# The output projection of a hybrid attention layer by Strassen's scheme, seven products for a pair of blocks

## Chip, cores and metric

One core of a Trainium2 chip runs the whole kernel. The metric is device time in microseconds; each engine (TensorE, VectorE, ScalarE, GpSimd, and SyncE, which issues the DMAs) runs its own list of instructions in order.

## What is computed

A decoder layer over 4096 tokens of width 1024. One input projection feeds two branches: sliding-window softmax attention (512 wide) and gated linear attention in chunks (512 wide). Both outputs, gated, stand side by side, go through the output projection, and the result is normalised with the residual:

```python
proj = einsum('bsd,de->bse', x, w_in)
out_a = sliding_window_attention(q_a, k_a, v_a, sinks) * silu(g_a)
o_b = gla_chunked(q_b, k_b, v_b, log_a)          # state carried along the sequence
out_b = rms_norm(o_b) * gla_norm_w * silu(g_b)
mix = einsum('bse,ed->bsd', concatenate([out_a, out_b]), w_out)   # 4096x1024 by 1024x1024
x = layer_norm(ALPHA * x + mix, ln_g, ln_b)
```

## The kernel before

The tokens are cut into 32 blocks of 128. Each matrix product runs on float32 values that are split in two float32r parts, high and low; a product is high by high, high by low and low by high, three matmuls for each 128 rows of the contraction (`project`, L135 to L137). `split` (L100 to L105) makes the parts: ScalarE or GpSimd copies the high part, VectorE or GpSimd subtracts it from the value.

The kernel has three stages, each a loop over the blocks.

The first projects and computes sliding-window attention; `a_out` stores the gated result of a block, transposed, in DRAM (half 0 of `mixd`).

The second computes gated linear attention. In an iteration n it projects block n (bq, bv, bk, bg) and finishes block n-1 between the projections (`b_attn`, `b_state`, `b_update`, `b_out`, `b_store`); `b_store` puts the transposed result in half 1 of `mixd`. VectorE and ScalarE have many short instructions here and GpSimd a few. Its four weight groups lie in SBUF, loaded and split by `load_group` near the end of the first stage, the k columns early in it. In the last iteration the two halves of w_o take the places of the v and g groups: 16 pieces, loaded, copied by ScalarE and subtracted by VectorE or GpSimd.

The third stage is the output projection. For each block it loads the two halves from `mixd` and the residual rows xr, splits (mh, ml), multiplies by the two column halves of w_o (two products py of 24 matmuls of 128x512 each, into PSUM banks that go round in two pairs), and evacuates each half on VectorE with the residual added (y, L756) and statistics taken (L757). Then come the aggregate (L758), the reciprocal root in `rsqrt_eps` (L780 to L785, with ScalarE's Ln and Exp between), the negated mean nb (L771), normalisation on ScalarE (L772), multiplication by ln_g on GpSimd (L773), addition of ln_b on VectorE (L774), and the store. The last block does its final arithmetic on VectorE in two halves (L766, L767).

The order of instructions on each engine is not that of the text alone. A planner takes the program once before it runs, and gives each engine, whenever it is free by the planner's own durations, the ready instruction that stands earliest in the text. What it writes is the order in which the engine then runs, whatever the true durations are; an instruction that waits stops all behind it on its engine. DMAs go through SyncE's one queue in the same manner. Tiles with one tag share a fixed number of buffers (`bufs`); a tile's first writer waits for the last reader of the buffer's earlier use. A PSUM bank is one such buffer of 128x512.

## Time and profile before

| | |
|---|---|
| Median of 3 runs | 1752.09 us (1750.44 to 1753.18) |
| Profiled execution | 1752.42 us, span of its instructions 1750.6 us |
| Busy in the span | TensorE 98%, VectorE 63%, ScalarE 48%, GpSimd 26% |
| Output projection, by the profile | first matmul at 1386.1 us, last at 1742.4 |
| DMA | 120.13 MB, mean 69 GB/s |

A row of the profile names the time or busy time in us, the engine (PE is TensorE's matmul, PEld its weight load, DVE VectorE, ACT ScalarE, POOL GpSimd, SPq SyncE's queue), the line of the kernel, the operation, and the tiles written and read. In brackets stands the idle time of the engine just before, and who ended it. The granted clock is TensorE's, 1.00 for 2.4 GHz. Matmuls are pipelined: a row of 0.39 us does not mean that the next one starts 0.39 us later.

### The profile page before, as it was taken

What the parts mean: (1) busy time and instruction counts of PE and PEld (TensorE: products, weight loads), DVE (VectorE), ACT (ScalarE), POOL (GpSimd) and SP (SyncE); (2) the same over time, 40 slices, a digit from 0 to 9 for tenths busy, and PEclk for the clock granted to TensorE, in tenths of its full rate; (3) what the DMA queues carried; (4) which work ended last, traced back from release to release, by engine and by line L of the source; (5) the groups of instructions that cost most, each with busy time, mean ns of one, the idle gap of its engine ahead of it and who ended that gap; (6) DMA issues with size and microseconds to landing.
All of it is one profiled execution on the core that took longest, in us unless ns stands there. A gap on an engine that the chain in (4) does not pass through costs nothing.

```text
span 1750.6 us, 27011 instructions
## 1 busy us (share of the span) xinstructions
PE 1716.2 (98%) x9722; PEld 1474.6 (84%) x9722; DVE 1094.8 (63%) x2802; ACT 847.9 (48%) x2128; POOL 456.6 (26%) x633
## 2 busy tenths in 40 slices
PE   7999999999999998999999999999999899999998
PEld 6788888888888887888888888888888788888886
DVE  6766666666666677566665565565556755555555
ACT  5555555455555556555555555555555622222221
POOL 3222222222222244322222222222222412222221
PEclk9999999999999999999999999999999899999999
DMA  6211111111111123111111111111111444444442
GB/s 204 91 37 37 37 37 37 43 49 37 37 37 37 37 73 105 37 37 37 38 37 37 37 37 37 37 40 41 37 37 37 156 139 145 144 145 144 145 144 84
DMA packets 65674, 120.13 MB, mean 69 GB/s; under 512 B 22658, under 2 KB 26116, under 8 KB 65540
## 3 DMA queue, kind: packets, MB, share of 16 engines
q1 hardware_dynamic: 65540, 118.41, 20.4%
q8 instruction: 76, 1.25, 0.3%
q14 instruction: 58, 0.48, 0.1%
HBM read 84.76 MB, written 33.62 MB: 68 GB/s over the span
## 4 chain that ended last, share of the span: by engine, by line
PE 57%; DVE 1%; ACT 0%; issue 0%; DMA 0%; POOL 0%; DVEq 0%; POOLq 0%; ACTq 0%
PE py L137 7%; PE py L135 7%; PE py L136 7%; PE bg L135 3%; PE bg L137 3%; PE bg L136 3%; PE bv L135 3%; PE bv L136 3%; PE bv L137 3%; PE bq L135 2%; PE bq L137 2%; PE bq L136 2%; PE bk L137 2%; PE bk L136 2%; PE bk L135 2%; PE to L679 1%
## 5 line engine op out<-in xcount | busy, mean ns | idle before, releaser
L135 PE MATMUL py<-wh,mh 128*128 128x512 f32 x512 | 200.4, 391 | 0.0
L137 PE MATMUL py<-wh,ml 128*128 128x512 f32 x512 | 200.4, 391 | 0.0
L136 PE MATMUL py<-wl,mh 128*128 128x512 f32 x512 | 200.3, 391 | 0.0
L341 POOL TENSOR_SCALAR s<-s,rec 128x256 f32<-128x256 f32 x256 | 123.8, 499 | 280.5 <-DVE ngm L329 217.3
L333 ACT ACTIVATE s<-s,ngm 128x256 f32<-128x256 f32 x256 | 127.2, 498 | 137.7 <-DVE ngm L329 132.9
L773 POOL TENSOR_TENSOR y<-y,lg 128x1024 f32<-128x1024 f32 x31 | 74.2, 2394 | 268.9 <-ACT y L772 253.5
L102 POOL TENSOR_SCALAR xh<-xraw 128x512 fp32r<-128x512 f32 x126 | 79.0, 643 | 229.2 <-PE pg L136 192.0
L316 DVE CUSTOM_DVE_ANT_0 s<-psc,msk 128x256 f32<-128x256 f32 x256 | 98.0, 420 | 31.6 <-PE psc L306 30.6
L105 DVE TENSOR_TENSOR pl<-pt,ph 128x512 fp32r<-128x512 f32 x128 | 85.7, 689 | 50.2 <-ACT ph L100 47.6
L137 PEld LDWEIGHTS py<-wh,ml 128*128 128x128 f32 x512 | 96.8, 189 | 20.0
L136 PEld LDWEIGHTS py<-wl,mh 128*128 128x128 f32 x512 | 96.8, 189 | 20.0
L135 PE MATMUL pg<-wh,xh 128*128 128x512 f32 x256 | 112.8, 440 | 0.8 <-DVE vv L249 0.8
L135 PEld LDWEIGHTS py<-wh,mh 128*128 128x128 f32 x512 | 96.8, 189 | 19.8
L100 ACT CAST ph<-pt 128x512 fp32r<-128x512 f32 x128 | 72.1, 589 | 85.0 <-PE pt L355 83.2
L527 POOL TENSOR_TENSOR qp<-bqs,ee 128x256 f32<-128x256 f32 x32 | 23.6, 738 | 337.3 <-ACT ee L524 324.0
L135 PE MATMUL pq<-wh,xh 128*128 128x512 f32 x256 | 104.9, 410 | 6.1 <-ACT wh L100 6.0
L100 ACT CAST mh<-mr 128x1024 fp32r<-128x1024 f32 x32 | 33.7, 1053 | 154.1 <-PE py L136 154.1
L135 PE MATMUL bg<-wh,xh 128*128 128x512 f32 x256 | 107.2, 419 | 0.0
L137 PE MATMUL pq<-wh,xl 128*128 128x512 f32 x256 | 103.4, 404 | 3.1 <-DVE xl L105 3.1
L135 PE MATMUL bv<-wh,xh 128*128 128x512 f32 x256 | 103.8, 405 | 0.0
L136 PE MATMUL pq<-wl,xh 128*128 128x512 f32 x256 | 103.0, 402 | 0.1
L136 PE MATMUL bv<-wl,xh 128*128 128x512 f32 x256 | 101.0, 395 | 0.0
(221 smaller groups left out, 5077.0 us busy)
## 6 DMA issues: line engine op xcount, KB each, us to landing
xraw<-in_xt_dram SPq DMA_DIRECT2D x64, 512.0 KB
mr<-mx SPq DMA_DIRECT2D x64, 256.0 KB
xr<-in_xn_dram SPq DMA_DIRECT2D x32, 512.0 KB
out_dram<-y SPq DMA_DIRECT2D x31, 512.0 KB
mx<-att SPq DMA_DIRECT2D x32, 256.0 KB
mx<-mb SPq DMA_DIRECT2D x32, 256.0 KB
wraw<-in_w_a_dram SPq DMA_DIRECT2D x16, 256.0 KB
wraw<-in_w_b_dram SPq DMA_DIRECT2D x16, 256.0 KB
```

The lines of the kernel that those rows point to most:

```text
L100: act.copy(hdst, src)
L102: pool.tensor_scalar(hdst, src, 1.0, 1.0, ALU.mult, ALU.mult)
L105: leng.tensor_tensor(ldst, src, hdst, ALU.subtract)
L135: pe.matmul(dst[:, :n], a, hs[k][:, :n], start=(k == 0), stop=False)
L136: pe.matmul(dst[:, :n], a, ls[k][:, :n], start=False, stop=False)
L137: pe.matmul(dst[:, :n], b, hs[k][:, :n], start=False, stop=(k == NK - 1))
L316: dve.tensor_tensor_reduce(out=s, in0=psc[:, e * 256 : (e + 1) * 256], in1=mask, scale=0.125, scalar=NEG, op0=ALU.add, op1=ALU.max, accum_ ...
L333: act.activation(sc[i], sc[i], AF.Exp, bias=ngm[:, h : h + 1], accum_out=den[:, h : h + 1])
L341: pool.tensor_scalar(sc[i], sc[i], rec[:, h : h + 1], 1.0, ALU.mult, ALU.mult)
L527: pool.tensor_tensor(qp, B[n]["q"], ee, ALU.mult)
L679: pe.transpose(to[:, hs], og[:, hs], ident)
L773: pool.tensor_tensor(y, y, lg, ALU.mult)
```

## The change

Two blocks of 128 tokens form a pair, the two halves of the contraction (attention branch, linear branch) and the two column halves of w_o the other sides of a 2x2 scheme. Seven products of 12 matmuls replace eight. With A11, A12 for the first block's halves and A21, A22 for the second's, the operands are A11, A12 and A22 as stored, and A11 - A21, A21 + A22, A22 - (A11 - A21) and A12 - (that). The seven right sides are blocks of w_o and four differences of them.

The row combinations are made in the second stage: `b_store` loads A11 and A21 back, VectorE makes the four combinations, and seven operands for each pair are stored (`opd`). The weight combinations are made there too, in `w_prepare`, in 8 batches after every third iteration: split into high and low parts and stored in DRAM (`wod`). In the last iteration and after it `w_fetch` brings the 28 split pieces (512 KB each) from there; no w_o split is left in it.

The third stage runs over pairs. Products 0, 1, 2 and 5 accumulate in one bank (`ba`), 3 and 6 in a second (`bb`), 4 in a third (`bc`), each with two buffers. VectorE reads a bank between the products that add to it, and adds each reading to the rows y that it belongs to (`plus`): y[0] low half from `ba` and `bc`, and so on, seven readings. Operands of the next pair are split in the text after each reading. The addition of ln_b runs on GpSimd for a pair's first block, on VectorE for its second.

To make room, weight groups are held as one tile of both parts, the q and k columns form one group of 528 columns loaded at the end of the first stage (the early load of k is gone), and buffers of the second stage are merged (r0 with lt, qp with ee, kp with ff, og with om, one gw).

```diff
-        wr = pa.enter_context(tc.tile_pool(name="wra", bufs=6))
+        wr = pa.enter_context(tc.tile_pool(name="wra", bufs=5))
...
-                wb["q"] = load_group(wr, w_b, 0, 272, 1, 272)
-            if n == 2:
-                wb["k"] = load_group(wr, w_b, 272, 256, 3, 256)
+                wb["qk"] = load_group(wr, w_b, 0, 528, 1, 528)
...
@@ b_store
-            mb = b1.tile([P, 512], F32, tag="mb", name=f"mb{n}")
-            act.copy(mb, to)
-            sp.dma_start(mixd[n][1].rearrange("p a s -> p (a s)"), mb)
+            p, odd = divmod(n, 2)
+            a2 = b1.tile([P, 512], F32, tag=f"mb{odd}", name=f"mb{n}")
+            act.copy(a2, to)
+            sp.dma_start(opd[p][4 + odd], a2)
+            if not odd:
+                a11 = b1.tile([P, 512], F32, tag="a11", name=f"a11_{p}")
+                a21 = b1.tile([P, 512], F32, tag="a21", name=f"a21_{p}")
+                sp.dma_start(a11, opd[p][0])
+                sp.dma_start(a21, a21d[p])
+                B[n]["a"] = a11, a21, a2
+                return
+            a11, a21, a12 = B[n - 1]["a"]
+            dve.tensor_tensor(a11, a11, a21, ALU.subtract)
+            sp.dma_start(opd[p][2], a11)
+            dve.tensor_tensor(a21, a21, a2, ALU.add)
+            sp.dma_start(opd[p][3], a21)
+            s2 = b1.tile([P, 4, P], F32, tag="om", name=f"s2_{p}").rearrange("p a s -> p (a s)")
+            dve.tensor_tensor(s2, a2, a11, ALU.subtract)
+            sp.dma_start(opd[p][1], s2)
+            dve.tensor_tensor(a12, a12, s2, ALU.subtract)
+            sp.dma_start(opd[p][6], a12)
+
+        def w_prepare(k, c):
...
+            def part(i, src):
+                w = b1.tile([P, 2, 256], F32R, tag="wo", name=f"wop{i}_{k}{c}")
+                split(w[:, 0], w[:, 1], src, act, dve)
+                sp.dma_start(wod[i][k][:, :, 256 * c : 256 * c + 256], w.bitcast(F32))
+
+            part(0, r11)
+            dve.tensor_tensor(r11, r12, r11, ALU.subtract)
+            dve.tensor_tensor(r12, r22, r12, ALU.subtract)
+            part(6, r22)
+            dve.tensor_tensor(r22, r22, r11, ALU.subtract)
+            part(3, r11)
+            part(4, r21)
+            dve.tensor_tensor(r21, r21, r22, ALU.subtract)
+            part(2, r12)
+            part(1, r22)
+            part(5, r21)
...
             if last:
-                wo[0] = load_group(wr, w_o, 0, 512, 0, 512)
+                w_fetch(0)
+                w_fetch(3)
...
+            if n % 3 == 2 and n < 26:
+                w_prepare(n // 6, n // 3 % 2)
...
@@ third stage
+        def product(dst, w, i, more=False):
+            h_, l_ = w[i]
+            for k in range(4):
+                h, l = wo[i][k][:, 0, :512], wo[i][k][:, 1, :512]
+                a, b = h_[:, k * P : (k + 1) * P], l_[:, k * P : (k + 1) * P]
+                pe.matmul(dst, a, h, start=(not more and k == 0), stop=False, skip_group_check=more)
+                pe.matmul(dst, a, l, start=False, stop=False, skip_group_check=more)
+                pe.matmul(dst, b, h, start=False, stop=(k == 3), skip_group_check=more)
...
             act.activation(y, y, AF.Identity, bias=nb_, scale=rs)
             pool.tensor_tensor(y, y, lg, ALU.mult)
-            dve.tensor_tensor(y, y, lb, ALU.add)
+            late.tensor_tensor(y, y, lb, ALU.add)
             sp.dma_start(out[rows, :], y)
...
+            product(ba, w, 0)
+            plus(y0, LO, ba, True)
+            ahead(0)
+            product(bb, w, 3)
+            plus(y1, HI, bb, True)
+            ahead(3)
+            product(ba, w, 1, more=True)
+            plus(y0, HI, ba, True)
+            ahead(1)
+            product(bc, w, 4)
+            plus(y0, LO, bc, False)
+            dve.bn_stats(st0[:, 0, :], y0[:, LO])
+            ahead(4)
+            product(ba, w, 2, more=True)
+            plus(y1, HI, ba, False)
+            dve.bn_stats(st1[:, 1, :], y1[:, HI])
+            ahead(2)
+            product(bb, w, 6, more=True)
+            plus(y0, HI, bb, False)
+            dve.bn_stats(st0[:, 1, :], y0[:, HI])
+            normed(n0, y0, st0, pool)
+            ahead(6)
+            product(ba, w, 5, more=True)
+            plus(y1, LO, ba, True)
+            dve.bn_stats(st1[:, 0, :], y1[:, LO])
+            ahead(5)
+            normed(n1, y1, st1, dve, final)
```

## Rows read from the trace of the kernel before

**Rows 1.** The profile page, its head and part 1: busy time, share, instructions.

```profile
span 1750.6 us, 27011 instructions
...
PE 1716.2 (98%) x9722; PEld 1474.6 (84%) x9722; DVE 1094.8 (63%) x2802; ACT 847.9 (48%) x2128; POOL 456.6 (26%) x633
```

**Rows 2.** Busy by stretch: stretch, length, PE, PEld, DVE, ACT, POOL, clock, DMA, GB/s.

```profile
740.00:1350.00 610.00, 610.00 (x3796) 538.85 (x3795) 368.65 (x881) 334.93 (x822) 153.37 (x196) 1.00 0.12 37
...
1416.20:1742.60 326.40, 326.40 (x1441) 270.20 (x1439) 177.05 (x359) 79.89 (x119) 71.82 (x30) 1.00 0.41 140
```

**Rows 3.** One block of the projection in order of time: start, length, engine, line.

```profile
1568.39 0.39 PE L135 MATMUL py<-wh,mh 128*128 128x512 f32 x1
...
1568.59 0.69 DVE L756 SCALAR_TENSOR_TENSOR y<-xr,py 128x512 f32<-128x512 f32 x1 [1.17 <-PE py L137]
...
1569.31 0.69 DVE L757 BATCH_NORM_STATS2 cst<-y 128x6 f32<-128x512 f32 x1
...
1569.92 1.21 DVE L105 TENSOR_TENSOR ml<-mr,mh 128x1024 fp32r<-128x1024 f32 x1
...
1571.05 0.20 DVE L758 BATCH_NORM_AGGREGATE mv<-cst 128x2 f32<-128x12 f32 x1
...
1571.94 0.16 DVE L783 TENSOR_TENSOR cnt<-crs 128x1 f32<-128x1 f32 x1 [0.50 <-ACT crs L782]
...
1572.72 1.24 ACT L772 ACTIVATE y<-y,nb,crs 128x1024 f32<-128x1024 f32 x1 [0.81 <-DVE nb L771]
...
1574.03 0.69 DVE L756 SCALAR_TENSOR_TENSOR y<-xr,py 128x512 f32<-128x512 f32 x1 [1.35 <-PE py L137]
...
1574.04 2.39 POOL L773 TENSOR_TENSOR y<-y,lg 128x1024 f32<-128x1024 f32 x1 [8.49 <-ACT y L772]
...
1576.46 1.23 DVE L774 TENSOR_TENSOR y<-y,lb 128x1024 f32<-128x1024 f32 x1 [1.75 <-POOL y L773]
...
1577.60 0.69 DVE L757 BATCH_NORM_STATS2 cst<-y 128x6 f32<-128x512 f32 x1
```

**Rows 4.** Order of time, VectorE and GpSimd late in the linear attention stage.

```profile
1373.02 1.30 POOL L105 TENSOR_TENSOR wl<-wraw,wh 128x512 fp32r<-128x512 f32 x1 [3.22 <-ACT wh L100]
...
1373.29 0.42 DVE L497 SCALAR_TENSOR_TENSOR la<-pz,lt 128x256 f32<-128x256 f32 x1 [0.24 <-ACT lt L452]
...
1374.87 0.16 DVE L784 SCALAR_TENSOR_TENSOR nt<-nt,ms 128x4 f32<-128x4 f32 x1
...
1375.36 1.39 POOL L105 TENSOR_TENSOR wl<-wraw,wh 128x512 fp32r<-128x512 f32 x1 [1.04 <-ACT wh L100]
...
1375.55 1.22 DVE L785 SCALAR_TENSOR_TENSOR rs<-nt,rs 128x4 f32<-128x4 f32 x1
```

**Rows 5.** Busy by stretch, columns as in rows 2, around the change of stage.

```profile
1375.00:1378.00 3.00, 1.09 (x4) 0.74 (x4) 2.88 (x8) 0.90 (x2) 1.39 (x1) 0.81 0.58 184
...
1378.00:1381.00 3.00, 3.00 (x11) 2.42 (x10) 1.37 (x4) 2.36 (x7) 0.67 (x1) 0.63 0.56 201
...
1395.00:1400.00 5.00, 5.00 (x14) 3.78 (x14) 1.87 (x5) 1.79 (x5) 0.53 (x1) 0.50 0.94 351
```

**Rows 6.** TensorE in order of time, the last block of the linear attention stage.

```profile
1361.16 0.39 PE L137 MATMUL bv<-wh,xl 128*128 128x512 f32 x1
...
1369.75 0.39 PE L137 MATMUL bv<-wh,xl 128*128 128x512 f32 x1
```

**Rows 7.** Groups of instructions, 700 to 1360 us: count, busy us, mean ns, idle before.

```profile
L105 DVE TENSOR_TENSOR al<-am,ah 128x512 fp32r<-128x512 f32 x30 | 20.3, 678 | 0.8 <-ACT ah L100 0.8
...
L105 DVE TENSOR_TENSOR lal<-la,lah 128x256 fp32r<-128x256 f32 x31 | 13.0, 420 | 0.9 <-ACT lah L100 0.9
...
L100 ACT CAST kph<-kp 128x256 fp32r<-128x256 f32 x31 | 12.6, 407 | 6.5 <-DVE kp L552 6.5
```

**Rows 8.** VectorE's end of the kernel in order of time.

```profile
1742.67 0.69 DVE L756 SCALAR_TENSOR_TENSOR y<-xr,py 128x512 f32<-128x512 f32 x1 [1.45 <-PE py L137]
...
1746.20 1.42 DVE L767 SCALAR_TENSOR_TENSOR y<-y,crs,lb 128x512 f32<-128x512 f32 x2
```

More of the change, by code (lines that the diff above doesn't have):

```diff
@@ new lines, in w_prepare @@
+        def w_prepare(k, c):
+            q = []
+            for i in range(2):
+                for j in range(2):
+                    r = wr.tile([P, 256], F32, tag="wraw", name=f"wo{k}_{c}{i}{j}")
+                    sp.dma_start(r, w_o[k + 4 * i, :, 512 * j + 256 * c : 512 * j + 256 * c + 256])
+                    q.append(r)
+            r11, r12, r21, r22 = q
+            def part(i, src):
[13 more added lines that the diff above has]
+            part(5, r21)
@@ new lines, in layer_kernel, with ahead, plus @@
+        for i in ORDER:
+            split_op(w_next, i)
+        for p in range(NB // 2):
+            n0, n1 = 2 * p, 2 * p + 1
+            w, (y0, y1), final = w_next, ys_next, p == NB // 2 - 1
+            if not final:
+                w_next, ys_next = load_pair(p + 1), load_rows(p + 1)
+            st0 = c2.tile([P, 2, 6], F32, tag="st0", name=f"cst{n0}")
+            st1 = c2.tile([P, 2, 6], F32, tag="st1", name=f"cst{n1}")
+            ba, bb, bc = bank("pj", f"pa{p}"), bank("c", f"pb{p}"), bank("d", f"pc{p}")
+            def ahead(i):
+                if not final:
+                    split_op(w_next, i)
+            def plus(y, s, b, first):
+                if first:
+                    dve.scalar_tensor_tensor(y[:, s], y[:, s], ALPHA, b, ALU.mult, ALU.add)
+                else:
+                    dve.tensor_tensor(y[:, s], y[:, s], b, ALU.add)
+            product(ba, w, 0)
[25 more added lines that the diff above has]
+            normed(n1, y1, st1, dve, final)
```

139 lines of the change are left out of this document (86 added, 53 removed).

## The prediction, written before the changed kernel ran

> **What bounds the kernel now.** I read the page's first part, then busy time by stretches. TensorE is busy 98% of the 1750.6 us span [rows 1], and in both stretches that the change touches (the middle of the linear attention stage, and the output projection from its third block on) it is busy all the time at full clock, with VectorE at 60% and 54% and the DMA engines at 0.12 and 0.41 [rows 2]. In the projection 326.40 us hold 1441 matmuls: 0.2267 us each, 48 to a block, so 10.88 us a block and 21.76 us a pair of blocks. The projection is limited by the number of matmuls, as long as nothing on the other engines is late.
>
> Then I read one block in order of time [rows 3]. Three things are to be seen there. First, the chain behind a product: the evacuation starts 0.20 us after the next product's first matmul (1568.59 against 1568.39); statistics, aggregate, scale and ScalarE's normalisation follow; GpSimd's multiplication by ln_g starts at 1574.04. Without the 1.13 us that the split ml takes between them (1569.92 to 1571.05) that is 4.3 us after the evacuation began, so 4.5 us after the product. Second, GpSimd needs 2.39 us for 128x1024, where VectorE's addition of the same shape takes 1.23. Third, VectorE stands idle for 1.75 us before that addition, though the statistics of the next half could run; they come after it, at 1577.60. The planner that wrote VectorE's order took GpSimd to be done by the end of the evacuation at 1574.72, after well under 2 us, not 2.39. Today nobody waits for VectorE here: each half has a PSUM bank of its own and four banks go round.
>
> Last, VectorE against GpSimd [rows 4]: a tiny instruction with both inputs in SBUF (128x4; its like took 0.16 us at 1374.87), started inside a GpSimd operation, ended with it: 1.22 us, until 1376.77 against GpSimd's 1376.75. One with an input in PSUM (128x256) ran through in its 0.42 us.
>
> **Removed and added, part by part.** *TensorE.* Seven products of 12 matmuls for a pair instead of eight: 84 x 0.2267 = 19.04 us, 2.72 a product; 16 pairs save 192 matmuls, 43.5 us. This is the most that the change can give.
>
> *VectorE in the projection.* For a pair: 7 evacuations and 4 statistics at 0.69, 7 splits at 0.60 (half of ml), 10 small ones at 0.16, 2 aggregates at 0.20, one addition at 1.23: about 15.0 us of 19.04, 79% [rows 3]. It fits by sum. GpSimd gets three operations of 2.39 (both multiplications, and the first block's addition, which moves there from VectorE), 7.2 us. ScalarE has 7 copies at no more than 0.62 and two normalisations at 1.24, under half.
>
> *The new waits.* Bank ba takes products 0, 1, 2 and 5, and VectorE must read it between each two. So product 1 waits for the reading after product 0, and product 2 for that after product 1; one other product (2.72 us) lies between, of which the reading takes 0.7. VectorE issues strictly in order, so whatever stands ahead of these readings stops TensorE. I follow one pair, with time 0 at the end of product 6. The first block's chain puts its multiplication on GpSimd at 4.5 and, right behind it, its addition from 6.9 to 9.3. The second block's last product ends at 2.72; its statistics reach the small two-input instructions at about 4.7, inside GpSimd's multiplication. By [rows 4] one gets through between the two operations, the others after 9.3. Normalisation on ScalarE starts at about 10.0, GpSimd's third operation runs from 11.4 to 13.8, VectorE's last addition to 14.95, and if the reading after product 1 stands behind that addition it ends at 15.65. Product 2 then starts at 15.75, where TensorE alone would be ready at 13.6; with products 2 and 6 the circle closes after 15.75 + 5.44 = 21.2 us. The reading after product 0 stands in the planner's order near the same small instructions; if behind them, it ends at 10.8, product 1 starts 2.7 us late, and product 2 cannot come before 16.3: 21.8 us. An evacuation or split ahead of the last addition adds 0.6 to 1.2. A stall of such length also has a price in clock: after the gaps between 1375 and 1378, with 1.09 us of TensorE work in 3 us, the granted clock stood at 0.81 and then 0.63, partly at the lower of the two levels, 1.2 GHz [rows 5]. I take 22.0 us a pair, within 21.2 to 23.5; the lower end of everything is 19.04, if no order does harm. Is the addition ahead of the reading? By the planner's belief it is ready about one GpSimd operation after the normalisation, some 2 us before product 1 ends; and it has the earlier place in the program. I take that as likely. For 15 pairs: 15 x (22.0 - 21.76) = **+3.6 us** (-8 to +26; without stalls 15 x -2.72 = -41).
>
> *Start of the projection.* Splits of w_o (16 pieces) vanish from the end of the linear attention stage; instead 28 pieces of 512 KB, 14.7 MB, are fetched into places that come free piece by piece while the last block's bv, bk and bg are multiplied. The fastest stretch moved 351 GB/s [rows 5]: 42 us for the weights, and some 3 to 4 MB of operands and rows, 9 to 12 us. The first place is free after the first bv block, at about 1362 [rows 6]; from there the transfers end at 1409 to 1416, and product 5 of the first pair at 1412 to 1419. Before, the first two blocks were through at 1742.6 - 326.4 = 1416.2. So the first pair ends where two blocks ended: **0** (-4 to +3). What was lost there before (splits, a low clock) pays for the wait for weights.
>
> *Row sums and weight combinations in the linear attention stage.* For a pair of blocks four VectorE operations of 0.68, and eight times a batch of 7 splits (ScalarE 0.41, VectorE 0.42 each) and four combinations of 0.42 [rows 7]: 2.7 us in two iterations, and 4.6 us on VectorE in one. An iteration takes about 21.5 us (30 to 31 of a kind in 660 us), of which 60% or 13.0 us are taken; the fullest one has 13.0 + 1.4 + 4.6 = 19.0 us. By cover it is free. Without it: the batch goes through one buffer, each piece waiting for the store of the last, and an instruction that waits stops its engine. Nothing shows what slack TensorE's order has there. Bounds: 0, and half a microsecond for each of 32 iterations plus 1 us for each batch, 24 us. I take **+5**, near the lower end, since [rows 2] shows a stage without a gap at 60% load.
>
> *Change of stage before it.* The second weight group grows from 272 to 528 columns and its 256 k columns come no longer early: 1 MB more at 351 GB/s is 3 us, and longer splits. **+2** (0 to +5). The merged buffers (r0, qp, kp, og, gw) are each rewritten only after their last reader of one iteration earlier: nothing.
>
> *End.* Before, from the last evacuation to VectorE's end: 1742.67 to 1747.62 [rows 8]. The last block now has its small and its final two-input instructions against the GpSimd operations of the block before, which run until 9.3 - 2.7 = 6.6 us after the last product, where the chain of before had ended 5.2 us after it; the rest is about 2.7 us of instructions behind them: about **+4** (0 to +5).
>
> Sum against the profiled execution's 1752.42 (span 1750.6 and 1.8 around it; the median 1752.09 is 0.3 lower): 1752.4 + 3.6 + 0 + 5 + 2 + 4 = **1767 us**.
>
> **Rivals.** *A: TensorE stays the bound.* For it: 79% of VectorE's time by sum, and no proof in the trace of where the planner puts the two readings. It needs both readings ahead of the blocked instructions. Then a pair takes 19.04 to 19.5: -41 to -34, with +3 to +9 for the other terms: 1714 to 1728. From the Trainium skill, Perfetto Trace Analysis, section Identifying the Most-Contended Engine: the engine with the highest occupancy is the one to relieve first. By that rule this rival would be the forecast, since no other engine comes near TensorE. The trace agrees with the rule for the kernel before and cannot show it for an order in which banks are handed back and forth.
>
> *B: only one of the readings is late, or the second block's small instructions slip in before GpSimd's first operation.* Then the circle is 13.8 less one GpSimd turn and closes at about 20 to 21: -26 to -11, with +7 for the others: 1733 to 1748.
>
> *C: VectorE becomes the bound, with splits standing in the blocked stretch too.* 15.0 us of work and up to three GpSimd operations waited out (7.2) are 22.2; with a lower clock after each stall 23 to 24: +19 to +34 and +11 for the rest: 1782 to 1797. It decides from 21.8 us a pair upwards.
>
> *D: the scheme takes away nothing.* Excluded, since the matmuls are counted: 84 for 96.
>
> *E: the weights arrive late.* With operands queued behind all the weights the first pair could end 10 us later than taken; this shifts each case and is in the range.
>
> **From these to the numbers.** My forecast (21.2 to 22.9 us a pair and +4 to +11 for the rest: 1748 to 1781) 0.45; A 0.24; B 0.13; C 0.18. A measurement of this kernel can tell 0.2%, 3.5 us. A and B are faster (B at its end just so), C slower, and of my own case most is slower, a little of it the same or faster: faster 0.38, same 0.09, slower 0.53. The range that leaves out a tenth at each side reaches from A to C: 1716 to 1792; my own case alone has 1748 to 1781.
>
> **What would show it.** In the profile after: TensorE's first matmul of products 1 and 2 waiting for VectorE once in each pair, by 2 to 3 us; pairs 21 to 23 us apart; VectorE's small scale instructions of the second block stretched to the end of a GpSimd operation; a granted clock below 1.00 in the projection; VectorE's addition of ln_b waiting for GpSimd by more than 1.75 us; 14.7 MB more read near 1365 to 1415 at about 350 GB/s; the linear attention stage still free of gaps outside the batches. I am wrong if pairs are 19 us apart (rival A: the order puts the readings first), or if the linear attention stage loses more than 24 us, or if the first pair ends far from 1416.

## The result and the profile after

The changed kernel takes 1855.37 us (median of 4 runs, 1852.47 to 1856.94; the first of these is the profiled one) against 1752.17 us (4 runs, 1750.44 to 1753.18): 1.0588 times as long, interval 1.057 to 1.0607. The prediction was 1767 us, 1716 to 1792: the direction was right, the size far off.

Two marks cut both spans into the same stretches: the transposes tr, one in each iteration of the linear attention stage (the first and the last stand 31 iterations apart), and the first matmuls of product 4, one in each pair. A pair's length is the mean of the last 14 distances between the latter; before, it is 21.76 us by count. The third row is the time from the last tr to the end of the last product, less 15 pairs. Times in us:

| stretch | before | after | difference | predicted |
|---|---|---|---|---|
| up to the first tr | 702.5 | 702.2 | -0.3 | +2 |
| 31 iterations of linear attention | 661.2 | 698.2 | +37.0 | +5 |
| start of the projection, with one pair's time | 52.4 | 58.0 | +5.6 | 0 |
| 15 pairs | 326.4 | 15 x 25.30 = 379.5 | +53.1 | +3.6 |
| behind the last product | 8.2 | 12.8 | +4.6 | +4 |
| span | 1750.6 | 1850.7 | +100 | +15 |

The page's head and part 1 of the kernel after, which answer to [rows 1]:

```profile
span 1850.7 us, 27675 instructions
...
PE 1716.2 (93%) x9530; PEld 1455.6 (79%) x9530; DVE 1272.0 (69%) x3054; ACT 886.7 (48%) x2240; POOL 498.9 (27%) x637
```

Busy time by stretch, columns as in [rows 2]. TensorE, without a gap before in both stages, now has 96% and 85%, and the projection a lower granted clock:

```profile
740.00:1350.00 610.00, 586.56 (x3582) 509.53 (x3582) 420.52 (x959) 332.06 (x825) 160.31 (x188) 1.00 0.30 97
...
1600.00:1700.00 100.00, 84.94 (x339) 68.08 (x338) 73.31 (x126) 28.85 (x53) 28.61 (x12) 0.91 0.47 158
```

One pair in the projection, VectorE in order of time, the answer to [rows 3, 4]. Product 6 has just ended (its reading is the first row):

```profile
1764.29 0.69 DVE L897 TENSOR_TENSOR y<-y,pb 128x512 f32<-128x512 f32 x1 [1.17 <-PE pb L840]
...
1769.44 0.15 DVE L864 SCALAR_TENSOR_TENSOR nb<-mv,crs 128x1 f32<-128x1 f32 x1
1769.73 0.69 DVE L895 SCALAR_TENSOR_TENSOR y<-y,pa 128x512 f32<-128x512 f32 x1
1771.06 2.36 DVE L935 TENSOR_TENSOR cnt<-crs 128x1 f32<-128x1 f32 x1 [0.64 <-ACT crs L934]
1773.45 0.16 DVE L936 SCALAR_TENSOR_TENSOR cnt<-cnt,mv 128x1 f32<-128x1 f32 x1
1773.65 2.25 DVE L937 SCALAR_TENSOR_TENSOR crs<-cnt,crs 128x1 f32<-128x1 f32 x1
...
1779.83 1.23 DVE L867 TENSOR_TENSOR y<-y,lb 128x1024 f32<-128x1024 f32 x1 [2.53 <-POOL y L866]
1780.98 0.68 DVE L895 SCALAR_TENSOR_TENSOR y<-y,pa 128x512 f32<-128x512 f32 x1
```

TensorE at the end of product 6 (the first matmul of product 5) and at the start of product 2:

```profile
1764.09 0.39 PE L838 MATMUL pa<-wo,oh 128*128 128x512 f32 x1
...
1781.80 0.47 PE L838 MATMUL pa<-wo,oh 128*128 128x512 f32 x1 [3.83 <-DVE y L895]
...
1786.22 0.40 PE L838 MATMUL pb<-wo,oh 128*128 128x512 f32 x1
```

GpSimd in the same stretch:

```profile
1771.01 2.39 POOL L866 TENSOR_TENSOR y<-y,lg 128x1024 f32<-128x1024 f32 x1 [17.40 <-ACT y L865]
1773.48 2.40 POOL L867 TENSOR_TENSOR y<-y,lb 128x1024 f32<-128x1024 f32 x1
1777.45 2.35 POOL L866 TENSOR_TENSOR y<-y,lg 128x1024 f32<-128x1024 f32 x1 [1.57 <-ACT y L865]
```

And TensorE's waits from 1500 us to the end (us in total, times, longest):

```profile
PE pa L838 <- DVE y L895: 54.3, 14, 6.5
```

It is the circle of the prediction. Two of the second block's scale instructions, 0.16 us each when nothing runs beside them, end with GpSimd's operations (1771.06 + 2.36 = 1773.42 against 1773.40). VectorE then waits 2.53 us for the third operation, with the reading after product 1 (1780.98) behind the addition; product 2 cannot start. TensorE waits 54.3 / 14 = 3.9 us a pair. Seven products without a wait are 84 x 0.2287 = 19.21 us (the distance that a run below reaches in 14 pairs out of 15). So 25.30 is 19.21 + 3.9 + 2.2, and the remaining 2.2 us are what the granted clock costs: it is 0.90 to 0.91 in the mean, since after each stop some matmuls run at the lower level, 1.2 GHz. In this pair product 2 takes 4.42 us (1781.80 to 1786.22) where the prediction's rate gives 2.72, and the granted clock reads 0.61 there.

In the linear attention stage: groups of GpSimd's and of VectorE's instructions from 700 to 1400 us. Before, the two groups of GpSimd had a mean of 738 and 729 ns. Of the four row sums one is slowed, the last (1069 ns; the other three keep 678 to 692):

```profile
L532 POOL TENSOR_TENSOR ee<-bqs,ee 128x256 f32<-128x256 f32 x31 | 30.2, 973 | 338.3 <-ACT ee L530 324.5 <-issue 13.8
L112 POOL TENSOR_TENSOR kpl<-ff,kph 128x256 fp32r<-128x256 f32 x31 | 29.1, 940 | 2.4 <-ACT kph L107 2.4
```

```profile
L704 DVE TENSOR_TENSOR mb<-mb,s 128x512 f32<-128x512 f32 x15 | 16.0, 1069 | 0.3
```

TensorE's waits in 740 to 1350 us, where [rows 2] had none:

```profile
PE bo L659 <- POOL sbl L551: 9.6, 13, 0.8
PE tb L564 <- POOL ee L532: 7.1, 16, 1.7
PE tr L490 <- DVE r L483: 4.2, 18, 0.5
```

The weight batches do not come after every third iteration, as the text of the kernel has them. The planner's order runs all eight one behind another: SyncE issues their first store at 710 us and their last at 981, in iteration 12. So the 31 iterations fall into three parts, by the distances between the transposes tr. Iterations 0 to 2 take 60.4 us instead of 56.6, iterations 3 to 12, with most of the batches, 233.4 instead of 215.6, and the 18 behind the batches 404.4 instead of 389.0: +3.8, +17.8 and +15.4.

The end, which answers to [rows 8]: the last block's scaling and its first final operation are held by GpSimd's work on the block before, as was reckoned:

```profile
1840.22 2.62 DVE L859 SCALAR_TENSOR_TENSOR y<-y,mv,lg 128x512 f32<-128x512 f32 x1
1842.75 2.29 DVE L935 TENSOR_TENSOR cnt<-crs 128x1 f32<-128x1 f32 x1
```

### The profile page after: what moved, and what is told of

It is laid out like the page before. It is cut to its first block, busy times and chain, and to the rows that moved or that the text cites. A ratio compares the mean times of both kernels' runs of the same rounds, so it can differ in the third digit from the quotient of the medians.

```text
span 1850.7 us, 27675 instructions
## 1 busy us (share of the span) xinstructions
PE 1716.2 (93%) x9530; PEld 1455.6 (79%) x9530; DVE 1272.0 (69%) x3054; ACT 886.7 (48%) x2240; POOL 498.9 (27%) x637
## 4 chain that ended last, share of the span: by engine, by line
PE 25%; DVE 12%; DMA 7%; POOL 6%; issue 6%; ACT 3%; SPq 1%; DVEq 0%; ACTq 0%; POOLq 0%
POOL y L866 3%; DMA wod<-wop 2%; POOL y L867 2%; PE pa L838 2%; PE bv L145 2%; PE bv L144 2%; PE bv L143 2%; PE pa L840 1%; PE pa L839 1%; DMA a<-a 1%; DMA ol<-op 1%; PE bg L143 1%; PE bg L144 1%; PE bg L145 1%; PE bk L144 1%
## 5 line engine op out<-in xcount | busy, mean ns | idle before, releaser
L143 PE MATMUL pg<-w,xh 128*128 128x512 f32 x256 | 112.9, 441 | 1.2 <-DVE vv L257 1.2
L838 PE MATMUL pa<-wo,oh 128*128 128x512 f32 x128 | 61.3, 479 | 53.3 <-DVE y L895 52.1
L143 PE MATMUL pq<-w,xh 128*128 128x512 f32 x256 | 103.9, 406 | 7.1 <-ACT w L107 6.0
L143 PE MATMUL bg<-w,xh 128*128 128x512 f32 x256 | 106.0, 414 | 0.0
L143 PE MATMUL bv<-w,xh 128*128 128x512 f32 x256 | 103.3, 403 | 0.0
L145 PE MATMUL pq<-w,xl 128*128 128x512 f32 x256 | 101.6, 397 | 0.6 <-DVE xl L112 0.6
L144 PE MATMUL pq<-w,xh 128*128 128x512 f32 x256 | 101.7, 397 | 0.1
L145 PE MATMUL pg<-w,xl 128*128 128x512 f32 x256 | 101.0, 394 | 0.0
L144 PE MATMUL pg<-w,xh 128*128 128x512 f32 x256 | 100.8, 394 | 0.0
L145 PE MATMUL bv<-w,xl 128*128 128x512 f32 x256 | 100.7, 393 | 0.0
L144 PE MATMUL bv<-w,xh 128*128 128x512 f32 x256 | 100.7, 393 | 0.0
L145 PE MATMUL bg<-w,xl 128*128 128x512 f32 x256 | 100.3, 392 | 0.0
L144 PE MATMUL bg<-w,xh 128*128 128x512 f32 x256 | 100.2, 392 | 0.0
L112 DVE TENSOR_TENSOR xl<-xraw,xh 128x512 fp32r<-128x512 f32 x128 | 85.0, 702 | 10.3 <-ACT xh L107 5.0
```

The costliest lines, as they stand in the source:

```text
L112: leng.tensor_tensor(ldst, src, hdst, ALU.subtract)
L143: pe.matmul(dst[:, :n], a, hs[k][:, c], start=(k == 0), stop=False)
L144: pe.matmul(dst[:, :n], a, ls[k][:, c], start=False, stop=False)
L145: pe.matmul(dst[:, :n], b, hs[k][:, c], start=False, stop=(k == NK - 1))
L838: pe.matmul(dst, a, h, start=(not more and k == 0), stop=False, skip_group_check=more)
```

## The experiments

A run for which one time is given was executed once. The stretch up to the first tr, where its code is unchanged, lies between 702.2 and 706.2 us in these runs, so that totals are good to some 4 us; lengths within a stage are read from the traces.

### The pair

**The addition behind the reading.**

```diff
-            late.tensor_tensor(y, y, lb, ALU.add)         # second block
...
             r1 = plus(y0, HI, ba, True)                   # product 1, next pair
+            after(dve.tensor_tensor(yp, yp, lb, ALU.add).ins, r1.ins)
```

> VectorE's addition of ln_b for a pair's second block is issued behind the reading after product 1 of the next pair, instead of ahead of it; all work and every bank stays. Theory (order): product 2 waits only because that reading stands behind the addition, which waits for GpSimd. The reading of bank ba then comes at the end of product 1, product 4 covers it, and a pair takes 19.0 to 19.6 us instead of 25.15 (first pairs aside); 15 pairs save 83 to 92 us, so 1763 to 1772 us, with a granted clock near 1.00 in the projection. Rival (VectorE is full: 73% busy, with small instructions held up by GpSimd): the stall only moves to another reading, a pair takes 23 us or more, 1823 us or more. Rival (the clock is low in this stage whatever waits): about 0.90 stays and a pair takes 21 us, 1793 us.

Measured: 1825.62 us, 23.16 us a pair. The order alone was worth 2.1 us, so the theory of order was right on a part only, and the rival (the stall moves) was right for the rest. VectorE in this run:

```profile
1590.38 2.40 DVE L830 TENSOR_TENSOR ol<-ol,oh 128x512 fp32r<-128x512 f32 x1 [0.94 <-ACT oh L829]
1592.70 2.35 DVE L942 TENSOR_TENSOR cnt<-crs 128x1 f32<-128x1 f32 x1
...
1596.18 0.68 DVE L897 SCALAR_TENSOR_TENSOR y<-y,pa 128x512 f32<-128x512 f32 x1
1599.41 1.23 DVE L912 TENSOR_TENSOR y<-y,lb 128x1024 f32<-128x1024 f32 x1 [2.54 <-POOL y L866]
```

GpSimd's operations end at 1592.22 and 1595.03 there. A split of 0.69 us is held until the first of them ends and then does its work; a scale instruction of 0.16 us ends with the second. The reading after product 1 comes 3.75 us late all the same (1596.18; product 4 had begun at 1592.43). Then the addition, now next, waits 2.54 us for GpSimd, with splits and the reading after product 2 behind it. TensorE waits twice, 1.64 and 1.67 us in this pair, and the granted clock is 1.00 from 1600 us on.

**One GpSimd operation fewer, the order kept.** Both additions on VectorE, and `after(r1.ins, add1.ins)`.

> The first block's addition of ln_b runs on VectorE instead of GpSimd, and the order of the suspected pair is kept by force: the reading after product 1 still stands behind the second block's addition. Theory (the circle of waits passes through every GpSimd operation, each with its 2.4 us, because VectorE's small two-input instructions end only with it): one GpSimd operation fewer in the circle, so product 2 starts 2.4 us earlier in each pair: 20.7 us by sum and up to 22.7 with the lower clock, 1779 to 1819 us. Rival (VectorE is full): 1.23 us more work on it for each pair, so a pair takes 25 to 26.4 us, 1853 to 1874 us.

Measured: 1845.08 us, 24.79 us a pair: neither. Only 0.5 us came back. VectorE in one pair:

```profile
1615.21 2.39 DVE L830 TENSOR_TENSOR ol<-ol,oh 128x512 fp32r<-128x512 f32 x1 [0.84 <-ACT oh L829]
1617.52 1.22 DVE L867 TENSOR_TENSOR y<-y,lb 128x1024 f32<-128x1024 f32 x1
...
1621.67 2.46 DVE L830 TENSOR_TENSOR oa<-oa,ob 128x512 fp32r<-128x512 f32 x1 [1.82 <-ACT ob L829]
1624.06 1.21 DVE L867 TENSOR_TENSOR y<-y,lb 128x1024 f32<-128x1024 f32 x1
```

The additions wait for nothing here. Ahead of each stands a split that is held as long as GpSimd multiplies (2.4 us instead of 0.69), so that each of the two multiplications still holds the order up.

**GpSimd's operations in quarters.**

```diff
-            pool.tensor_tensor(y, y, lg, ALU.mult)
+            for q in range(4):
+                s = slice(256 * q, 256 * q + 256)
+                pool.tensor_tensor(y[:, s], y[:, s], lg[:, s], ALU.mult)
```

> As the run with the addition behind, and GpSimd's multiplication and addition of a block are cut into four pieces of 256 columns each; the work is the same. Theory (lock: VectorE's two-input instructions on SBUF end only with the GpSimd instruction that runs beside them, 2.3 to 2.4 us in that run for the split and for the small scale instruction): each is now held for at most one piece, 0.6 us, so the two stalls of 2.0 us a pair shrink to under 1 us together: 19.3 to 21 us a pair instead of 23.1, 1763 to 1794 us. Rival (GpSimd's chain is long, whatever its pieces): 23 us a pair and 1822 us or more.

Measured: 1836.82 us, 23.60 us a pair: the expected gain did not come, though the instructions did what was expected of them:

```profile
1617.86 0.73 DVE L830 TENSOR_TENSOR ol<-ol,oh 128x512 fp32r<-128x512 f32 x1 [0.47 <-ACT oh L829]
1618.52 0.69 DVE L946 TENSOR_TENSOR cnt<-crs 128x1 f32<-128x1 f32 x1
1619.25 0.66 DVE L947 SCALAR_TENSOR_TENSOR cnt<-cnt,mv 128x1 f32<-128x1 f32 x1
...
1626.22 1.23 DVE L916 TENSOR_TENSOR y<-y,lb 128x1024 f32<-128x1024 f32 x1 [3.31 <-POOL y L868]
```

Held for 0.7 us instead of 2.4, the scale chain is through early, the reading after product 1 is in time, and the addition waits still longer, 3.31 us, with the reading after product 2 behind it. GpSimd itself became slower: four pieces took up to 3.29 us where the whole operation took 2.4:

```profile
1617.31 3.29 POOL L868 TENSOR_TENSOR y<-y,lg 128x256 f32<-128x256 f32 x4 [13.87 <-ACT crs L458]
```

**The addition behind that reading too** (`after(..., r2.ins)`):

> As the run with GpSimd's work in quarters, and VectorE's addition of ln_b for the second block is issued behind the reading after product 2 of the next pair instead of that after product 1. Theory (lock and order each cost on their own: with quarters the lock holds an instruction for 0.7 us at most, and what was left there was the addition, issued 3.3 us before GpSimd was done, with splits and two readings behind it): both gone, 19.0 to 20.0 us a pair instead of 23.5, 1780 to 1792 us. Rival (GpSimd's chain is too long wherever the addition stands): 22.5 us a pair and 1822 us or more.

Measured: 1823.33 us, 22.94 us a pair, a miss; the time is the rival's, but its cause is not what the trace shows. VectorE's waits from 1500 to 1800 us name the next in the row: splits that the planner had issued early, and whose ScalarE copies waited in turn for operands in transfer (56.3 us in 18 waits).

```profile
DVE oa L830 <- ACT ob L829: 68.0, 12, 6.8
```

**GpSimd out of the stage.**

```diff
-            act.activation(y, y, AF.Identity, bias=nb_, scale=rs)
-            pool.tensor_tensor(y, y, lg, ALU.mult)
-            late.tensor_tensor(y, y, lb, ALU.add)
+            dve.scalar_tensor_tensor(y, y, mv[:, 0:1], lg, ALU.subtract, ALU.mult)
+            dve.scalar_tensor_tensor(y, y, rs, lb, ALU.mult, ALU.add)
```

> GpSimd and ScalarE leave the normalisation: VectorE does it in two operations of 128x1024 for each block ((y - mean) x ln_g, then x scale + ln_b), so it has about 3.5 us more work in a pair, some 17.3 us of 19.04. Theory (lock and order): without GpSimd nothing is held up, the planner's durations are near the true ones, and a pair takes 19.1 to 20.5 us: 1763 to 1786 us. Rival (VectorE is full, its work sets the time): more work on it makes a pair longer than 25.15 us, 1856 us or more.

Measured: 1778.36 us, 20.04 us a pair, as the theory had it. The edit also moves these operations in the text, behind product 5 and the next product 0, so that lock and order are not told apart by it. VectorE has more work and TensorE waits less; by stretch:

```profile
1600.00:1700.00 100.00, 96.88 (x421) 78.18 (x420) 85.57 (x160) 25.13 (x55) 0.00 (x0) 1.00 0.61 197
```

**The reading after product 0 first** (`after(second operation of the first block, r0)`):

> As the run without GpSimd, and the first block's last operation on VectorE is issued behind the reading after product 0 of the next pair, which in that run came 2.8 us after the product, behind three operations of 1.27 us. Theory (order alone sets what is left, 1.07 us a pair at the start of product 1): no stall is left and a pair takes 19.0 to 19.2 us instead of 20.1, 1762 to 1765 us. Rival (VectorE at 87% is the bound now): the stall moves to another reading, 20 us a pair and 1776 us or more.

Measured: 1777.09 us, 19.94 us a pair: next to nothing. TensorE's waits behind that reading fell from 9.2 us to 4.7, but not the pair. In VectorE's waits stood splits, 15.1 us behind ScalarE's copies, and in ScalarE's these copies, 45.1 us behind operand transfers. **GpSimd at work beside, for nobody**, in that kernel:

```diff
+            for _ in range(3):
+                pool.tensor_tensor(dummy, w["b"].bitcast(F32), lg, ALU.mult)
```

> As the run with the reading first, and GpSimd gets back three multiplications of 128x1024 for each pair, which read a split operand and ln_g and write a buffer that nobody reads: it works beside, and no instruction waits for its result. Theory (lock: VectorE's two-input instructions on SBUF end only with the GpSimd instruction beside them): VectorE, 87% busy, loses 2 to 5 us of the 7.2 that GpSimd works in a pair, a pair takes 22 to 25 us instead of 20.0 and the kernel 1803 to 1842 us. Rival (GpSimd cost what it did only because VectorE waited for its results): 20.0 us a pair, 1774 to 1781 us.

Measured: 1821.00 us, 43.9 us more; 22.2 us a pair, 21.2 from the sixth on. Groups from 1560 to 1800 us:

```profile
L908 POOL TENSOR_TENSOR dummy<-ob,lg 128x1024 f32<-128x1024 f32 x30 | 79.1, 2638 | 138.0 <-ACT ob L831 136.5
L832 DVE TENSOR_TENSOR ol<-ol,oh 128x512 fp32r<-128x512 f32 x43 | 44.4, 1032 | 0.6 <-ACT oh L831 0.6
...
L902 DVE SCALAR_TENSOR_TENSOR y<-y,pa 128x512 f32<-128x512 f32 x35 | 23.7, 677 | 1.4 <-PE pa L842 1.4
```

Nobody reads `dummy`, and yet the splits (two inputs in SBUF) take 1032 ns in the mean instead of 688, while the readings (one input in PSUM) keep 677. So the lock has a price of its own, though a smaller one than the total: 33.5 of the 43.9 us lie in the first five pairs, where GpSimd ran nine of these multiplications in a row (23.9 us), and the ten pairs behind them lose 1.0 us each. The Trainium skill, SBUF — State Buffer, section Who interferes with whom, has this rule: a VectorE instruction with two SBUF inputs and a GpSimd instruction that reads SBUF exclude each other for the whole instruction. This trace agrees.

**Loads apart** (each operand of the pair after the next loaded right behind the product that frees its buffer):

> As the run with the reading first, and each operand of the pair after the next is loaded right behind the product that frees its buffer, instead of all seven in a row at the start of the pair before. Theory (what is left above 19.04 us a pair comes from SyncE's queue: loads stand behind row stores that wait up to 10 us for VectorE, so ScalarE's copies and VectorE's splits of operands run late): 19.0 to 19.4 us a pair instead of 20.0, 1762 to 1769 us. Rival (VectorE at 87% is the bound): 20 us a pair, 1774 us or more.

Measured: 1777.48 us, 20.01 us a pair: the theory fell as tried. The row stores still stood ahead of the loads in SyncE's order and waited for VectorE:

```profile
SPq L885 <- DVE mv L974: 67.3, 10, 8.2
```

What was left was the place of the splits. It was fixed in the last version: each split behind the reading that stands ahead of it in the text, with the loads apart, the sums and the weight pieces as tried below.

```diff
-                    split_op(w_next, i)
+                    after(split_op(w_next, i).ins, r.ins)
```

> Sums read from PSUM, two buffers for the weight pieces (split before they are stored, as in the changed kernel), the projection without GpSimd, the reading first, the loads apart, and now each split on VectorE is issued behind the reading that stands ahead of it in the text, not up to a pair earlier. Theory (what held a pair at 20.0 us was splits issued early, waiting in VectorE's order for operands still in transfer, with the reading after product 0 behind them): 19.1 to 19.4 us a pair; with the linear attention stage at 672 to 677 us, 1740 to 1752 us, at or just below the kernel before. Rival (VectorE at 87% is the bound): 20 us a pair, 1752 to 1764 us.

Measured: 1757.52 us (9 runs, 1754.77 to 1758.97), ratio to before 1.0028, interval 1.0018 to 1.0037: 0.3% slower. The last 14 pairs are 19.21 us apart, every one, and no wait of TensorE's is left in them:

```profile
1500.00:1600.00 100.00, 100.00 (x439) 82.01 (x438) 87.99 (x168) 24.81 (x55) 0.00 (x0) 1.00 0.63 209
1600.00:1700.00 100.00, 100.00 (x439) 82.03 (x438) 86.37 (x165) 26.87 (x58) 0.00 (x0) 1.00 0.64 210
```

So VectorE at 87% does not bound the pair; its order and GpSimd did. The pair of the prediction's rival A exists (19.21, 38.2 us won in 15), but this version is still no faster than before: its first tr comes at 708.7 (+6.2), its 31 iterations take 677.5 (+16.3), its start 69.0 (+16.6), its end 9.6 (+1.4).

### The linear attention stage

**Without the row sums** (the four combinations left out, the operands stored uncombined) and **without the weight work** (the splits and combinations of the batches left out, raw values stored):

```diff
-            dve.tensor_tensor(a11, a11, a21, ALU.subtract)      # and three more
...
-                split(w[:, 0], w[:, 1], src, act, dve)          # the other run
```

> The four row combinations of a pair (VectorE, two inputs in SBUF) are left out; the same seven operands are stored, uncombined, and the same loads are made. Theory (they collide with GpSimd's operations and delay VectorE's other work in the linear attention stage): the 31 iterations there lose 20 to 26 us of their 698, 1829 to 1836 us. Rival (the loads and stores of operands cost the time): within 4 us of 1855. Rival (the weight batches cost it all): the same, within 4 us.

> The weight batches keep their DMAs (the loads are 512 columns instead of 256, 1 MB for a batch instead of 0.5, the stores are the same), but ScalarE's copies and VectorE's subtractions and combinations are left out, so that raw values are stored. Theory (the work, in a single buffer, delays the stage in iterations 2 to 25): the linear attention stage gets 10 to 13 us shorter, 1842 to 1846 us. Rival (the transfers, 0.41 to 0.47 of the DMA engines there, cost it): no gain, 1853 us or more.

Measured: 1835.64 us, 31 iterations in 682.4 us (-15.8, less than the 20 to 26 expected), and those after the batches back at 21.5 us; 1841.52 us, 686.7 us (-11.5, as expected). Without the sums the 18 iterations behind the batches take 388.6 us (404.4 with them, 389.0 before): there the sums are the whole cost. Without the weight work the gain lies ahead of that, 8.9 us in iterations 3 to 12. Of the 37.0 us, 37.0 - 15.8 - 11.5 = 9.7 come back with neither run, all of them in the first 13 iterations, where sums and batches fall together. No run left out both, and no transfer was taken away in either, so the cause of these 9.7 us stays open.

**Two buffers for the weight pieces** (`b3`, bufs=2, for tag wo):

> The weight pieces in the linear attention stage get two buffers instead of one; all work stays. Theory (a piece waits for the store of the one before, and ScalarE and VectorE stop with it): of the 11.5 us that the work of the batches costs, 5 to 11 come back: 1844 to 1850 us, and iterations 2 to 24 take 22.3 to 23 us. Rival (the work itself, by its collisions with GpSimd and its place in the order, costs the time): within 3 us of 1855.

Measured: 1854.10 us; 31 iterations in 691.6 us (-6.6), with ScalarE's waits for the store of a piece down from 33.4 to 20.2 us. The gain is in the stage, but this run's first tr came 4.0 us later, and the total shows little.

**Sums from PSUM.**

```diff
-            dve.tensor_tensor(a21, a21, a2, ALU.add)
+            dve.tensor_tensor(a21, to, a21, ALU.add)      # to: the transposed block in PSUM
-            dve.tensor_tensor(s2, a2, a11, ALU.subtract)
+            dve.tensor_tensor(a11, to, a11, ALU.subtract)  # a11 - a21 is made in the stage before
-            dve.tensor_tensor(a12, a12, s2, ALU.subtract)
+            dve.tensor_tensor(u, u, to, ALU.subtract)      # u = to + a11 in the even block
```

> The row combinations are arranged so that VectorE has no two-input instruction on SBUF for them in the linear attention stage: the difference of the two attention halves is made in the stage before, and the other three sums read the transposed block in PSUM and one operand in SBUF (four instructions for a pair here, as many as now, one of them in the even block). Theory (lock): the iterations after the weight batches go back from 22.3 to 22.6 to 21.5 to 21.8 us, the stage is 12 to 16 us shorter: 1839 to 1843 us. Rival (four more instructions ahead of the others in VectorE's order cost it, whatever they read): iterations stay at 22.3 to 22.6 us and the time within 4 us of 1855.

Measured: 1838.86 us; 31 iterations in 676.7 us (-21.5), the later ones 21.87 us, a little above the theory. VectorE does as many sums in this stage as in the changed kernel, yet GpSimd's groups are back:

```profile
L539 POOL TENSOR_TENSOR ee<-bqs,ee 128x256 f32<-128x256 f32 x31 | 23.1, 746 | 336.0 <-ACT ee L537 324.3 <-issue 11.6
L112 POOL TENSOR_TENSOR kpl<-ff,kph 128x256 fp32r<-128x256 f32 x31 | 23.1, 744 | 6.1 <-ACT kph L107 5.9
```

and TensorE's wait for ee (7.1 us) is gone. Its wait for sbl is not, though it is nearly so without the sums (first line this run, second line the run without them):

```profile
PE bo L666 <- POOL sbl L558: 7.8, 14, 0.6
PE bo L659 <- POOL sbl L551: 1.1, 2, 0.7
```

The 18 iterations behind the batches show what is the lock's: 404.4 us in the changed kernel, 394.6 here, 388.6 without sums. So 9.8 of 15.8 us, some two thirds of the row sums' cost, go with reading both inputs in SBUF; the other 6.0 us stay with the sums, by their time or their place in VectorE's order. (One of the four sums also moved to the pair's even block, so that the place is not quite the same in both.) That this run gains more over all 31 iterations than the one without sums (21.5 against 15.8) lies in the first 13, where it also moved loads and changed buffers. The difference that moved stands in the stage before, which got longer: the first tr at 711.5 us, 5 us above the highest of the runs with unchanged code there.

**Weights stored and fetched unsplit** (four combinations for a batch, no split there; 28 splits after the fetch):

```diff
-                split(w[:, 0], w[:, 1], src, act, dve)         # w_prepare
...
+                split(h, l, raw, act, pool if k % 2 else dve)   # w_fetch
```

> Only the four weight combinations are made in the linear attention stage and stored as they are (no split there, 4 instead of 7 pieces); the three others are read from w_o. After the fetch each of the 28 pieces is split in its place, on ScalarE and on VectorE or GpSimd in turn, as w_o was before: 7.3 MB are fetched instead of 14.7. Theory (two terms: the batches' work costs 11.5 us in the linear attention stage, and the start is bound by the transfer of the weights, 42 us at 350 GB/s): the stage gets 7 to 11 us shorter and the first pair comes 8 to 20 us sooner after it: 1824 to 1840 us. Rival (the start waits for the last block's chain, not for weights): only the 7 to 11 us, 1844 to 1848 us.

Measured: 1849.37 us; 31 iterations in 687.4 us (-10.8), but the first product 4 came 58.8 us after the last tr instead of 48.6, with half the bytes to fetch. That the 28 splits stood in the way of the last block is likely, but not shown: with none of them on GpSimd, in the second run below, the first product 4 came no sooner (56.7 us after the last tr; 56.4 in the first). **Three edits together**, and **once more** with the loads apart and no split on GpSimd:

> Three edits together: sums read from PSUM, weights stored and fetched unsplit, and the projection without GpSimd with the reading first. Theory (the three terms of the loss lie in separate stages and add): about 1763 us of the run with the reading first, less 12 to 17 for the sums, less 15 to 30 for the weights: 1716 to 1736 us, faster than before. Rival (the terms share the same slack, so that each gives less beside the others): 1740 to 1752 us.

> As the run with three edits together, with the loads apart as well, and with the splits of fetched weights all on VectorE, none on GpSimd, where they held up the last block's chain (GpSimd 15 of 20 us busy there, a transpose 7.7 us late). Theory: 19.1 to 19.4 us a pair instead of 20.3 takes off 12 to 16 us, the start 3 to 8: 1741 to 1751 us, at or below the kernel before. Rival (VectorE is then full at the start): the start gives nothing back, 1750 to 1756 us.

Measured: 1765.54 us and 1764.80 us; 31 iterations in 675.0 and 671.3 us, 20.24 and 20.16 us a pair; both times lie above theory and rival. The terms did not add: beside the sums from PSUM the weight edit gave 2 to 5 us more in the stage, not 11.

### The start

**Half the weights' transfer** (only the high parts fetched and used in place of the low parts, which are left out).

```diff
-                sp.dma_start(w[:, :, :512].bitcast(F32), wod[i][k])
+                sp.dma_start(w[:, 0, :512].bitcast(F32), wod[i][k][:, 0])
```

> The changed kernel, fetching only the high part of each weight piece; the products use it in place of the low part too, which is thereby left out of the result. The number of matmuls and all else stays; 7.3 MB less are fetched. Theory (the start is bound by the transfer of the weights): the first pairs come 8 to 20 us sooner after the last block's projections, 1835 to 1847 us. Rival (the last block's chain and the buffers that come free only after it set the start): within 4 us of 1855.

Measured: 1847.33 us. The first product 4 comes 41.4 us after the last tr instead of 48.6, that of the third pair 86.9 instead of 93.7: half the transfer is worth 7 us, a little less than the theory. Something else counts beside it. In the changed kernel SyncE has issued 24 of the 28 weight pieces by 1428.3 us; then its queue waits for the last block's stores, and the loads of product 4's operands stand behind these:

```profile
1424.81 3.52 SPq L746 DMA_DIRECT2D wo<-wod  x7
1438.05 0.32 SPq L688 DMA_DIRECT2D op<-mb  x1
...
1443.18 1.75 SPq L824 DMA_DIRECT2D ol<-op  x4
```

TensorE waits 9.6 us for product 4's operand there, the longest wait of the start.

**The last block's chain first** (`after(first matmul of product 0, last transpose)`), against the last version:

> As the run before it, and TensorE's first product is issued behind the last transpose of the last block, instead of ahead of that block's chain. Theory (the loss at the start is a wait in order: product 0 waits for weights with the last block's matmuls behind it, and the buffers of the third stage, the rows y and product 4's operand among them, come free only when that block is stored): the last block ends sooner, product 4 no longer waits 9 us, and the first pair ends 8 to 18 us sooner: 1724 to 1742 us. Rival (the start is bound by the transfer of the weights alone): within 4 us of the run before it.

Measured: 1758.18 us (5 runs, 1756.77 to 1760.12), the same. TensorE's longest waits from 1385 to 1480 us, in the version without and with this edit:

```profile
PE pc L866 <- DMA ol<-op: 9.8, 1, 9.8
PE bo L666 <- ACT sbh L558: 6.2, 1, 6.2
```

```profile
PE bo L666 <- ACT sbh L558: 7.3, 1, 7.3
PE pc L868 <- ACT oh L859: 6.7, 1, 6.7
```

The last block waits for its own state, whoever goes first on TensorE, and product 4 still waits 6.7 us: the theory fell. By the table's count the start of the last version is 11 us longer than that of the changed kernel (69.0 against 58.0). Its first product 4 comes no later (46.4 us after the last tr against 48.6); the difference lies between the first and the second product 4, 30.8 us apart in the last version, whose later pairs take 19.21, and 23.8 in the changed kernel, whose later pairs take 25.30 in the mean. What holds the second pair up stays open.

## Why the prediction was wrong, point by point

**The circle of a pair: right mechanism, wrong size.** Product 2 waits for the reading after product 1, that stands behind the addition, and the addition behind three GpSimd operations that VectorE's small instructions cannot pass, as was written. The step that failed is "puts its multiplication on GpSimd at 4.5": it started 6.9 us after product 6 (1771.01 against 1764.09, product 5's first matmul), since the planner had filled the gaps of the chain with three splits, a reading and the second block's statistics. That is 2.4 us, of which the rest of the chain made up 0.4: product 2 began 17.71 us after product 6's end (1781.80), not 15.75. The second omission is the clock: the text gave rows for its fall but put no term into the 22.0 us. Products 2 and 6 took 7.15 us in this pair (1781.80 to 1788.95) instead of 5.44. So the 21.2 us of the text's first case become 21.2 + 2.0 + 1.7 = 24.9, the length of this pair; the mean is 25.30. The other case, a late product 1, did not come about in this pair: TensorE has no wait there. Rival C held both ingredients and stopped at 24. This term is 53.1 us instead of 3.6.

**"By cover it is free" failed in the linear attention stage.** The step took 60% load of VectorE as cover, +5 us, and bounds of 0 to 24; 37.0 were measured. What it counted was the sums' own time (0.68 us each), spread under that load, and a batch in every third iteration, which the planner's order did not keep. What the sums cost was for the greater part the lock, which [rows 4] showed and which the text applied to the projection alone: they slowed ee and kpl on GpSimd by 0.2 us each, one of them was slowed itself, and TensorE came to wait for what stands behind. Behind the batches, sums that read PSUM take back 9.8 of the 15.8 us that leaving the sums out takes back. The work of the batches is 11.5 us more, and 9.7 us stay open. With this term alone at its measured size and all others as forecast, the kernel would have taken 1799 us, outside the range already.

**The start** was put at 0 (-4 to +3) and cost 5.6. The reckoning that it is set by the weights' transfer was right in part (7 us for half of it); what it left out is the wait of SyncE's queue for the last block's stores, with product 4's operands behind them. By the mark that the text named, the end of the first pair, it is worse: some 70 us after the last tr (at 1470.05), where two blocks had ended 52.6 us after it. TensorE had done two products of the second pair by then, so that the table's count shows less.

**The end and the change of stage**: +4 against 4.6, and +2 against -0.3, which is within the spread of that stretch.

**Rival A** did not come about, but was possible: 19.21 us a pair. In its way stood no engine's load. The Trainium skill, Perfetto Trace Analysis, section Identifying the Most-Contended Engine, says to optimise the engine of highest occupancy first (for TensorE it goes by MFU and the weight loads' busy share, not by the matmuls'). Here VectorE had 73% and TensorE's weight loads 68%, and what helped was another order on VectorE with more work on it (86% and more), and none on GpSimd, at 29%. For a circle of waits the load did not tell what to change, and in that this trace does not agree with the rule.

## What to carry to other kernels

Where a bank goes back and forth between two engines, follow the in-order queue of each through one period with every filler that the planner may put between, and count each two-input instruction that another engine's lock can stretch; load tells nothing of it. Price "hidden" work by what it locks and what is queued behind it, not by its own time: the same sums with one input in PSUM cost a third as much behind the batches (5.6 us over the kernel before instead of 15.4). And add a scheme's side work before the scheme: here 43.5 us at most could be won, and with the projection at its floor the row sums, weights and start still gave all of it back.

## What was not expected of the hardware

Cutting GpSimd's operation of 2.4 us into quarters shortened the hold on each VectorE instruction to 0.7 us, but then every small instruction of the chain met one (four in a row, 0.66 to 0.69 us each, instead of two of 2.3). One stop and two had different clocks: with one of 3.9 us a pair the granted clock was 0.90 to 0.91, with two of 1.6 to 1.7 us it was 1.00 from 1600 us on.
